# In-projection of the last 1408 tokens in seven half-size products, weight sums kept in DRAM, modulation rows later, one stream of split weights

## The chip, the cores and the metric

The kernel runs on one core of one Trainium2 chip. The metric is the device time of one execution in microseconds (us). The core has TensorE (PE, matrix products into the on-chip accumulator memory PSUM), VectorE (DVE), ScalarE (ACT), GpSimd (POOL) and SyncE (SP), which here issues every DMA. Each engine works through its own queue in order. Data lie in DRAM and in SBUF, the on-chip memory of 128 partitions; PSUM has eight banks of 512 fp32 values in each partition.

## The reference

One layer with a short gated convolution and a bidirectional mLSTM side by side, then a convolutional FFN. 128 context tokens and 2048 latent tokens pass through the same weights, with shift, scale and gate (the modulation) from two conditioning vectors.

```python
def trunk_layer(x, mod, row_len, ffn_axis, C0, n0, m0, norm1, w_in, ...):
    shift1, scale1, gate1, shift2, scale2, gate2 = jnp.split(mod, 6, axis=-1)
    h = rmsnorm(x, norm1) * (1 + scale1) + shift1
    z = h @ w_in
    sc_b, sc_c, sc_x, q, k, v, o, g = jnp.split(z, idx, axis=-1)
    u = (sc_c * sc_x).reshape(B, rows, row_len, D_CONV)
    y_sc = sc_b * conv3(u, conv_sc_w, conv_sc_b, axis=2).reshape(B, T, D_CONV)
    h_m, C, n, m = mlstm_bidir(heads(q), heads(k), heads(v), gates, C0, n0, m0)
    h_m = ... * jax.nn.sigmoid(o)
    x = x + gate1 * (jnp.concatenate([y_sc, h_m], axis=-1) @ w_out)
    h2 = rmsnorm(x, norm2) * (1 + scale2) + shift2
    up = conv3((h2 @ w_up)..., conv_ffn_w, conv_ffn_b, axis=ffn_axis)
    x = x + gate2 * ((jax.nn.silu(gg) * a) @ w_down)
```

The width is 1024, so an in-projection is a product of 1024 by 3600 (seven parts of 512 columns and 16 gate columns). `mod` is a product of 1024 by 6144 for each conditioning vector. All of it is fp32 in and out.

## The kernel before

**Tokens.** The 2176 tokens stand in one row of columns, context first, in six blocks `BL` of 384 (the last has 256). `BA` are the blocks 0 to 2 (tokens 0 to 1151) and `BB` 3 to 5 (1152 to 2175).

**Products.** An fp32 operand is split into a high part that TensorE takes exactly and a low part, the rest. A product of 128 output rows is `gemm`: for each of eight slices of 128 of the inner dimension three matmuls, high by high, high by low and low by high, 24 in all, into one PSUM bank.

```python
            PE.matmul(acc[:, :n], w_h, hH[:, k, :n], start=(k == 0), stop=False)
            PE.matmul(acc[:, :n], w_h, hL[:, k, :n], start=False, stop=False)
            PE.matmul(acc[:, :n], w_l, hH[:, k, :n], start=False, stop=(k == KT - 1))
```

`load_w` reads a weight tile of 128 by 1024 (512 KB), ScalarE copies out its high part (L105) and VectorE subtracts for the low part (L108). Three banks take turns in `accumulator`. For the gates and v (`vg`, L338 to L340) the tokens are the stationary operand and 264 weight columns stream.

**Order of the work.** (1) The start: `mod_pe` computes modulation rows 0 to 15 (shift1 and scale1) with TensorE from 16 tiles of 512 KB (L467), block 3 is read and normalised. (2) `BB`: v and gates, k and q for four heads each, the short convolution (three products per group of 128 channels), at last o. Beside them run `first_stats` (the sums of squares of `BA`) and `mod_dve`: the modulation rows 16 to 47, each from 512 KB read and two products with a sum on VectorE over 1024 elements (L510). (3) `BA`: `make_h` normalises each block beside the o products of `BB`, then `vg` and k. The scans of the gates (`gate_phase`) run beside k. (4) `weave` walks over 34 units `Sums` (state sums, backwards over the 17 chunks of 128 tokens, for two pairs of heads) and then 34 units `Mix` (the mixing itself: line L793 is part of it). Between the steps of a unit it takes products from `fill`: q, o, the short convolution of `BA` and the out-projection of blocks 0 to 3, (1, 0, 1) products per `Sums` unit and (2, 1, 2) per `Mix` unit. What is computed (k, q, o, v, sums, y) goes through DRAM (`kD`, `qD`, `oD`, `vD`, `sD`, `yD`). (5) The last out-projections, with the token sums of the FFN beside them. (6) The FFN's up-projection and (7) its down-projection.

**Seven products.** The FFN's up-projection already uses a Strassen-Winograd scheme: two output tiles by two halves of the inner dimension form a 2 by 2 weight matrix (`a11` to `a22`), two token halves by the same two halves of the inner dimension a 2 by 2 token matrix, and seven half-size products replace eight. `weights` makes the seven weight operands with four sums on VectorE (L273) and splits each (`part`, L279 and L280). Token sums are made once (`sums`) and read back (`split`). Products 0 to 2 are copied out of their bank (L957); products 2, 3, 4 and 6 accumulate onto the bank that an earlier one left; the other results are added to the copies (L964). There each product runs over two token parts of 272 columns.

**Who sets the order.** The tile framework places semaphores and puts each engine's instructions into an order of its own, by its estimates of when they are ready; the order in the text is a priority. A buffer is waited for until its last user is through.

## Time and profile before

| | |
|---|---|
| median of 3 runs | 2571.7 us (2571.41 to 2576.62) |
| the profiled execution | 2576.51 us |
| its span, first to last instruction | 2574.4 us |
| granted TensorE clock, mean | 0.992 |
| up-projection, 1086 to 2016 us | PE busy 927.1 us |
| down-projection, 2016 to 2575 us | PE busy 542.2 us |
| HBM read, written | 305.1 MB, 95.0 MB |

The page gives busy times of each engine; matmuls overlap, so their busy durations are longer than the distance from one to the next. A line such as `L200 PE MATMUL acc<-hH,wh 128*128 128x384 f32 x1280 | 440.9, 344 | 0.0` is a group: line, engine, operation, output and inputs, shape, count, then busy us and mean ns of one, and the idle time of the engine just before them with what ended it. A window's line gives the stretch, its length, busy us and count of PE, weight loads, DVE, ACT and POOL, the granted clock, the share of the DMA engines and GB/s. A DMA's line gives the tile and its source, the count, the size of one and the median us from issue to landing.

### The profile page before, as it was taken

The numbers are of one execution on the slowest core, as the hardware profiler recorded it, in microseconds if no ns is written. First come the engines' busy times: TensorE is split into PE (matmuls) and PEld (weight loads), VectorE is DVE, ScalarE is ACT, GpSimd is POOL, SyncE is SP. The second block draws the span as 40 slices with busy tenths as digits, with TensorE's granted clock in tenths as the row PEclk, the third lists the DMA queues.
The fourth block names the chain that finished last, engine by engine and source line by source line (L and its number), as shares of the span: only waits on it lengthen the run. The fifth ranks groups of instructions, "written<-read, shape, count | busy, mean of one in ns | idle before, by whom it ended". The sixth has DMA issues, their size and how long they took to land.

```text
span 2574.4 us, 46544 instructions
## 1 busy us (share of the span) xinstructions
PE 2525.0 (98%) x18511; PEld 2506.9 (97%) x18511; DVE 1621.1 (63%) x3130; ACT 1054.1 (41%) x1994; POOL 64.3 (2%) x134
## 2 busy tenths in 40 slices
PE   8999999999999999999999999999999999999998
PEld 8999999999999999999999999999999999999998
DVE  4993252332677776797887789777777635353533
ACT  4521152332444444554554455455545523231411
POOL 0000000000011110000000000000000000000000
PEclk9999999999999999999999999999999999999999
DMA  8882142565567887853252224222221826354442
GB/s 281 280 253 76 58 147 87 162 205 181 170 205 235 278 247 235 292 175 106 89 185 84 86 103 149 87 84 84 84 84 67 285 84 216 126 179 156 149 143 69
DMA packets 223579, 403.22 MB, mean 157 GB/s; under 512 B 20722, under 2 KB 144770, under 8 KB 221698
## 3 DMA queue, kind: packets, MB, share of 16 engines
q1 hardware_dynamic: 223362, 400.25, 47.4%
q8 instruction: 145, 2.38, 0.4%
q14 instruction: 72, 0.59, 0.1%
HBM read 305.13 MB, written 95.04 MB: 155 GB/s over the span
## 4 chain that ended last, share of the span: by engine, by line
PE 87%; DMA 6%; DVE 4%; issue 1%; ACT 1%; POOL 0%; SPq 0%; DVEq 0%; ACTq 0%; POOLq 0%
PE acc L200 8%; PE acc L202 8%; PE acc L201 8%; PE d L1049 7%; PE pa L952 7%; PE d L1047 7%; PE pa L954 7%; PE d L1048 7%; PE pa L953 6%; PE pb L954 3%; PE pb L952 3%; PE pb L953 3%; PE pc L954 2%; PE pc L952 2%; PE pc L953 2%; PE y L721 1%
## 5 line engine op out<-in xcount | busy, mean ns | idle before, releaser
L200 PE MATMUL acc<-hH,wh 128*128 128x384 f32 (+1 forms) x1536 | 513.3, 334 | 0.0
L202 PE MATMUL acc<-hH,wl 128*128 128x384 f32 (+1 forms) x1536 | 504.7, 329 | 0.0
L201 PE MATMUL acc<-hL,wh 128*128 128x384 f32 (+1 forms) x1536 | 503.7, 328 | 0.0
L952 PE MATMUL pa<-tH,wh 128*128 128x272 f32 x1408 | 409.0, 291 | 3.8 <-DVE row L438 3.4
L954 PE MATMUL pa<-tH,wl 128*128 128x272 f32 x1408 | 407.8, 290 | 0.1
L1047 PE MATMUL d<-uh,wh 128*128 128x272 f32 x1408 | 404.3, 288 | 2.9 <-ACT uh L996 2.2
L953 PE MATMUL pa<-tL,wh 128*128 128x272 f32 x1408 | 405.7, 288 | 0.0
L1049 PE MATMUL d<-uh,wl 128*128 128x272 f32 x1408 | 405.4, 288 | 0.0
L1048 PE MATMUL d<-ul,wh 128*128 128x272 f32 x1408 | 403.6, 287 | 0.1
L200 PEld LDWEIGHTS acc<-hH,wh 128*128 128x128 f32 x1536 | 290.1, 189 | 1.4 <-issue 0.4
L201 PEld LDWEIGHTS acc<-hL,wh 128*128 128x128 f32 x1536 | 290.1, 189 | 0.7
L202 PEld LDWEIGHTS acc<-hH,wl 128*128 128x128 f32 x1536 | 289.7, 189 | 0.3 <-issue 0.2
L952 PEld LDWEIGHTS pa<-tH,wh 128*128 128x128 f32 x1408 | 265.6, 189 | 4.5 <-DVE row L438 3.6
L1047 PEld LDWEIGHTS d<-uh,wh 128*128 128x128 f32 x1408 | 265.5, 189 | 3.7 <-ACT uh L996 2.6
L953 PEld LDWEIGHTS pa<-tL,wh 128*128 128x128 f32 x1408 | 266.1, 189 | 0.0
L954 PEld LDWEIGHTS pa<-tH,wl 128*128 128x128 f32 x1408 | 265.3, 189 | 0.3 <-DVE wl L280 0.3
L1049 PEld LDWEIGHTS d<-uh,wl 128*128 128x128 f32 x1408 | 265.0, 188 | 0.1
L1048 PEld LDWEIGHTS d<-ul,wh 128*128 128x128 f32 x1408 | 263.9, 187 | 0.5 <-DVE ul L997 0.3
L900 DVE SCALAR_TENSOR_TENSOR tt<-raw,fw,tt 128x127 f32<-128x127 f32 (+4 forms) x264 | 242.4, 946 | 4.7 <-ACT tt L906 3.6
L1008 ACT ACTIVATE wh<-st 128x1408 fp32r<-128x1408 f32 x64 | 88.3, 1380 | 356.2 <-PE d L1048 196.2
L954 PE MATMUL pb<-tH,wl 128*128 128x272 f32 x704 | 203.8, 290 | 0.8 <-DVE wl L280 0.8
L1010 DVE TENSOR_TENSOR wl<-st,wh 128x704 fp32r<-128x704 f32 x128 | 108.3, 887 | 152.5 <-ACT wh L1008 152.4
(214 smaller groups left out, 4681.8 us busy)
## 6 DMA issues: line engine op xcount, KB each, us to landing
st<-in_w_up SPq DMA_DIRECT2D x88, 512.0 KB, 4.5
st<-in_w_down SPq DMA_DIRECT2D x64, 704.0 KB, 4.1
wst<-in_w_in SPq DMA_DIRECT2D x48, 512.0 KB, 4.2
us<-uD SPq DMA_DIRECT2D x88, 272.0 KB, 4.9
R<-nD SPq DMA_DIRECT2D x34, 512.0 KB, 5.2
wm<-in_w_modr SPq DMA_DIRECT2D x32, 512.0 KB, 5.1
F<-tD SPq DMA_DIRECT2D x12, 1088.0 KB, 6.2
uD<-tt SPq DMA_DIRECT2D x22, 576.0 KB, 2.8
```

The source lines that it names most:

```text
L200: PE.matmul(acc[:, :n], w_h, hH[:, k, :n], start=(k == 0), stop=False)
L201: PE.matmul(acc[:, :n], w_h, hL[:, k, :n], start=False, stop=False)
L202: PE.matmul(acc[:, :n], w_l, hH[:, k, :n], start=False, stop=(k == KT - 1))
L900: V.scalar_tensor_tensor(o, i, w, o, op0=ALU.mult, op1=ALU.add)
L952: PE.matmul(acc, wh[:, w], rh, start=(kk == 0 and i in (0, 1, 5)), stop=False, skip_group_check=True)
L953: PE.matmul(acc, wh[:, w], rl, start=False, stop=False, skip_group_check=True)
L954: mm = PE.matmul(acc, wl[:, w], rh, start=False, stop=(kk == 3), skip_group_check=True)
L1008: S.activation(wh, st, AF.Copy)
L1010: V.tensor_sub(wl[:, a:b], st[:, a:b], wh[:, a:b].bitcast(F32))
L1047: PE.matmul(acc[b][:, :NB], wh[:, c], uh[:, q], start=(j == 0), stop=False)
L1048: PE.matmul(acc[b][:, :NB], wh[:, c], ul[:, q], start=False, stop=False)
L1049: PE.matmul(acc[b][:, :NB], wl[:, c], uh[:, q], start=False, stop=(j == FT - 1))
```

## The change

The tokens are cut anew: `BA` is blocks 0 and 1 (tokens 0 to 767), and `GR` has two groups of two equal halves: group 0 is tokens 1408 to 2175 (halves of 384), group 1 tokens 768 to 1407 (halves of 320). In both groups the in-projection goes by the seven products of the up-projection; k of group 0 alone is computed directly, as its tokens come in one half after the other. `BA` stays direct. All products now take half the inner dimension at a time.

```diff
+GR = ((1408, 384), (768, 320))
-BA = (0, 1, 2)
-BB = (3, 4, 5)
+BA = (0, 1)
+    mD = dr.tile([7, P, 4, 384], F32, name="mD")
+    wD = dr.tile([12, 4, P, WP], F32, name="wD")
...
+    def half(acc, w, s, n, first, last):
+        (wh, wl), (sh, sl) = w, s
+        for kk in range(4):
+            c = slice(kk * P, (kk + 1) * P)
+            PE.matmul(acc, wh[:, c], sh[:, kk, :n], start=first and kk == 0, stop=False, skip_group_check=True)
+            PE.matmul(acc, wh[:, c], sl[:, kk, :n], start=False, stop=False, skip_group_check=True)
+            PE.matmul(acc, wl[:, c], sh[:, kk, :n], start=False, stop=last and kk == 3, skip_group_check=True)
```

The weight operands come from one generator, in the order in which the whole kernel uses them, up-projection included. It reads up to two units ahead, and `take` keeps three split operands ahead. In group 0 the four sums of a unit are written to DRAM (`wD`); in group 1 they are read from there.

```diff
+    def seven(a11, a12, a21, a22, save=None, load=None):
+        def add(op, i, a, b, t):
+            op(t, a, b)
+            if save is not None:
+                Q.dma_start(wD[save, i][:, :n], t)
+            return t
+        if load is not None:
+            s1, s2, s4, s3 = (tmp() for _ in range(4))
+            for i, t in enumerate((s1, s2, s4, s3)):
+                Q.dma_start(t, wD[load, i][:, :n])
+            for a in (a11, s1, s2, s4, s3, a12, a22):
+                yield part(a)
+            return
+        yield part(a11)
+        s1 = add(V.tensor_add, 0, a21, a22, tmp())
+        yield part(s1)
...
+    def take():
+        while len(feed) < 3:
+            w = next(weights, None)
+            if w is None:
+                break
+            feed.append(w)
+        return feed.pop(0)
```

`pair` computes two output tiles of a group: one bank per product chain, one half-product after the other.

```diff
+        def pair(g, emit, scale=1.0, after=None):
+            t0, n = GR[g]
+            bank, cp = {}, {}
+            for i in range(7):
+                kind = KIND[i]
+                if i in (0, 1, 5):
+                    bank[kind] = pab[kind != "a"].tile([P, 512], F32, name="a" if kind == "a" else "b")
+                acc = bank[kind][:, :n]
+                half(acc, take(), gs[ORDER[i]], n, i in (0, 1, 5), True)
+                if i < 3:
+                    cp[i] = row()[:, :n]
+                    S.activation(cp[i], acc, AF.Copy, scale=scale)
+                else:
+                    m, blk, other = PLACE[i]
+                    emit(m, blk, acc, cp.get(other))
+                if after:
+                    after(i)
+                yield
```

Token sums of group 0 are made in SBUF during the start, those of group 1 by `gsums` beside group 0 (VectorE, four steps) and written to `mD`; `refill` reads them back into the seven token slots during the last pair of group 0. `fill_h` does the like with the normalised `BA` blocks during the last pair of group 1. `mod_dve` (two buffers instead of five) leaves the start's memory and is asked for beside group 1, `values` (v of `BA`), k and `fill`. The start takes the first two weight units and normalises group 0 half by half:

```diff
+            x0 = load_half(0)
+            h0 = norm_half(0, x0)
+            next(h0)
             mods(2, 4)
...
+            next(h0)
+            next(h0)
+            k3 = first_heads()
+            run(islice(k3, 1))
             mods(4, 8)
...
+            next(h0)
+            run(islice(k3, 3))
+            x1 = load_half(1)
+            h1 = norm_half(1, x1)
+            next(h1)
+            run(islice(k3, 4))
...
+        side = chain(first_stats(((768, 384), (1152, 256))), gsums(1))
+        run(beside(chain(vg(0), heads(0, qD, None, QS), heads(0, oD, AF.Sigmoid)), side, 4, 1000))
+        conv = shortconv(0, refill(1))
+        run(beside(islice(conv, 35), side, 4, 1000))
+        run(side)
+        run(conv)
...
+        run(beside(chain(vg(1), heads(1, kD), heads(1, qD, None, QS), heads(1, oD, AF.Sigmoid)), side, 6, 20))
+        run(side)
+        scale_rows()
+        run(beside(shortconv(1, fill_h), side, 6, 20))
+        run(beside(values(), side, 6, 3))
```

The mixing takes half-products instead of products:

```diff
-        weave([Sums(c, hp) for c in range(NL - 1, -2, -1) for hp in range(2)], fill, (1, 0, 1))
-        weave([Mix(c, hp) for c in range(-1, NL) for hp in range(2)], fill, (2, 1, 2))
+            weave([Sums(c, hp) for c in range(NL - 1, -2, -1) for hp in range(2)], fill, (1, 1, 1, 1, 1, 1, 1, 1, 1, 2))
...
+        weave([Mix(c, hp) for c in range(-1, NL) for hp in range(2)], fill, (2, 3, 2, 3, 2))
```

Six PSUM banks serve the groups (three and three, taken in turn), three the direct products during the mixing, as before.

More of the change, by code (lines that the diff above doesn't have):

```diff
@@ L1 @@
 from contextlib import ExitStack
-from itertools import chain, count, islice
+from itertools import chain, count, cycle, islice
 import numpy as np
@@ new lines, in values, with two @@
+                        Q.dma_start(vD[t][:, 2 * j:2 * j + 2], r)
+                        V.tensor_add(gates[:, t, j * 8:(j + 1) * 8], acc[:, 256:264], bgate[:, j * 8:(j + 1) * 8])
+                    yield
+        def two(emit):
+            for m in range(2):
+                accs = [accumulator() for b in BA]
+                for kh in range(2):
+                    w = take()
+                    for b, acc in zip(BA, accs):
+                        half(acc[:, :384], w, hs[b, kh], 384, kh == 0, kh == 1)
+                        if kh:
+                            emit(m, b, acc[:, :384])
+                        yield
+                        while due:
+                            due.pop(0)()
@@ new lines, in first_stats, with beside @@
+        def first_stats(blocks):
+            for b0, w in blocks:
+                ss = ssp.tile([P, 384], F32, name="ss")
+                for k in range(KT):
+                    x = row()[:, :w]
+                    Q.dma_start(x, I["x"][k][:, b0:b0 + w])
+                    square(ss, x, w, k == 0)
+                    if k % 4 == 3:
+                        yield
+                inv_rms(ss, w, rcol(b0, w))
+                yield
+        md = mod_dve()
+        tick = count()
+        def beside(products, side, every, mods):
+            for _ in products:
+                i = next(tick)
+                if i % every == 0:
+                    next(side, None)
+                if i % mods == mods - 1:
+                    next(md, None)
+                yield
@@ L927, in hymba_kernel @@
         cv = iter(())
-        while ahead:
-            nxt = next(prods, None)
-            if nxt:
-                ahead.append(nxt)
-            hf, j, i, (wh, wl) = ahead.pop(0)
+        for hf, j, i in ((hf, j, i) for hf in range(2) for j in range(FT) for i in range(7)):
+            wh, wl = take()
             if i == 0:
```

785 lines of the change are left out of this document (494 added, 291 removed).

## The prediction

> **What bounds the kernel now.** I read the page first: busy times, the 40 slices, the chain of work that ended last.
>
> ```profile
> span 2574.4 us, 46544 instructions
> PE 2525.0 (98%) x18511; PEld 2506.9 (97%) x18511; DVE 1621.1 (63%) x3130; ACT 1054.1 (41%) x1994; POOL 64.3 (2%) x134
> ...
> PE 87%; DMA 6%; DVE 4%; issue 1%; ACT 1%; POOL 0%; SPq 0%; DVEq 0%; ACTq 0%; POOLq 0%
> ```
>
> TensorE is on 87% of the chain that ended last, DMA on 6%, VectorE on 4%. So a matmul taken out shortens the kernel unless something else is then late. Next the windows view by stage (columns: length, then busy us of PE, PEld, DVE, ACT, POOL, granted clock, DMA share, GB/s), cut where the lines of the timeline change.
>
> ```profile
> 0.00:43.00 43.00, 33.92 (x270) 33.71 (x271) 19.53 (x53) 14.09 (x23) 1.64 (x9) 0.96 0.83 299
> 43.00:100.00 57.00, 54.96 (x423) 53.56 (x422) 42.76 (x104) 37.63 (x79) 3.28 (x17) 0.97 0.79 255
> 100.00:194.00 94.00, 94.00 (x607) 94.00 (x606) 91.33 (x172) 23.73 (x42) 4.06 (x4) 1.00 0.82 266
> 346.00:421.00 75.00, 71.30 (x548) 71.12 (x548) 31.59 (x79) 31.45 (x69) 1.43 (x14) 0.98 0.36 114
> 825.00:980.00 155.00, 144.88 (x903) 143.79 (x902) 112.70 (x340) 70.69 (x203) 17.84 (x32) 0.94 0.83 255
> 980.00:1086.00 106.00, 100.73 (x666) 100.09 (x665) 78.30 (x172) 50.38 (x102) 4.37 (x6) 0.98 0.84 274
> 1086.00:2016.00 930.00, 927.08 (x7344) 925.58 (x7343) 752.76 (x1123) 489.84 (x833) 0.44 (x1) 1.00 0.32 110
> ```
>
> TensorE idles 9.1 us in the start (43.0 − 33.9, DMA at 299 GB/s), 2.0 while it runs in, 3.7 where the last 1024 tokens hand over to the first 1152, 10.1 where the mixing units and the out-projection run together (DMA share 0.83, clock 0.94), 5.3 at the hand-over to the FFN, and 2.9 in the FFN's 930 us, which is already done in seven half-size products. In 100 to 194 VectorE is busy 91.3 us of 94 (it does the modulation rows there) and TensorE still never stops.
>
> A busy duration doesn't give the price of a matmul, since they overlap. The price is the distance between starts. One line's own view gives count, first and last start; three matmuls pass per record of a line.
>
> ```profile
> L201 PE MATMUL acc<-hL,wh x29: 334/334/343, 342.2 to 356.9; 128*128 128x384 f32 x29
> ```
> ```profile
> L201 PE MATMUL acc<-hL,wh x31: 274/283/285, 359.1 to 369.8; 128*128 128x256 f32 x31
> ```
> ```profile
> L338 PE MATMUL acc<-wh,hH x56: 281/282/290, 391.0 to 410.9; 128*128 128x264 f32 x56
> ```
>
> 14.7 us / (28 × 3) = 175.0 ns for 384 columns, 10.7 / (30 × 3) = 118.9 for 256, 19.9 / (55 × 3) = 120.6 for 264. Between the first two that is 0.438 ns a column, so 320 columns should cost 118.9 + 64 × 0.438 = 147.0 ns. Columns are what is paid for, and the weight load hides.
>
> **The change part by part.** The matmul counts of before:
>
> ```profile
> L200 PE MATMUL acc<-hH,wh 128*128 128x384 f32 x1280 | 440.9, 344 | 0.0
> ...
> L338 PE MATMUL acc<-wh,hH 128*128 128x264 f32 x272 | 79.0, 291 | 3.7 <-DVE gates L345 3.7
> ...
> L200 PE MATMUL acc<-hH,wh 128*128 128x256 f32 x256 | 72.4, 283 | 0.0
> ```
>
> *Matmuls.* A quarter of L200 is the out-projection (8 of 32 output tiles). That leaves 960 × 3 = 2880 of 384 columns and 192 × 3 = 576 of 256 for the in-projection: 2880 × 0.1750 + 576 × 0.1189 = 572.5 us. After: the first 768 tokens directly, 24 tiles × 24 × 2 blocks = 1152; k of the last 768 tokens directly, 4 × 24 × 2 = 192; the other ten pairs of tiles there, 10 × 7 products × 12 = 840; and twelve pairs for tokens 768 to 1407, 12 × 7 × 12 = 1008, of 320 columns. 2184 × 0.1750 + 1008 × 0.1470 = 530.4. v and the gates fall from 272 × 3 = 816 to 288 + 252 + 252 = 792 matmuls of 264 columns, 24 × 0.1206 = 2.9 us. **Together −45.0 us**, with every matmul on a path that TensorE sets.
>
> *Work of VectorE and ScalarE.*
>
> ```profile
> L280 DVE TENSOR_TENSOR wl<-s,wh 128x512 fp32r<-128x512 f32 x176 | 120.6, 686 | 6.1 <-ACT wh L279 2.6
> ```
> ```profile
> L510 DVE SCALAR_TENSOR_TENSOR jk<-wm,cB x64: 1222/1228/1235, 73.8 to 192.9; 128x1024 f32<-128x1024 f32 x64
> ```
> ```profile
> L380 DVE TENSOR_TENSOR cr<-acc,cr 128x384 f32<-128x384 f32 x20 | 11.1, 556 | 66.4 <-PE acc L202 66.4
> ```
> ```profile
> L279 ACT ACTIVATE wh<-s 128x512 fp32r<-128x512 f32 x176 | 111.0, 631 | 170.5 <-PE pc L953 95.0 <-PE pa L953 52.2 <-PE pb L953 18.8
> ```
> ```profile
> L377 ACT ACTIVATE cr<-acc 128x384 f32<-128x384 f32 x20 | 9.7, 483 | 52.7 <-PE acc L202 52.7
> ```
>
> A pair of 384 columns gives TensorE 7 × 12 × 0.175 = 14.7 us. VectorE does 7 splits and 4 weight sums of 512 in it (11 × 0.686) and 3 additions out of PSUM (3 × 0.556): 9.2 us, 63%; ScalarE 7 × 0.631 + 4 × 0.483 = 6.3. With the sums read back from DRAM (the 640-token group) VectorE saves 4 × 0.686 = 2.7 per pair. The short convolution adds six passes to a gated pair (3.3) and four to an output pair (2.2); statistics and token sums of the next group are 46 passes once, about 23. All this lies beside matmuls: cost 0 as long as VectorE isn't full. If that cover is gone, it is a rival below. The modulation rows, 64 × 1.228 = 79 us, leave the start's memory and queue. Line L510 began at 73.8 us, though the text issues these steps beside the q products far later: the framework starts what has its buffers. So I expect them to fill VectorE's gaps in both groups again. Their 32 reads of 512 KB move behind the first group's weights in SyncE's queue and stand there among a pair's 1 MB of weights, four saved sums of 256 KB and four stores of 192 KB: 2.9 MB in 14.7 us, 196 GB/s, below the 307 worked out further down. Weights are read up to two pairs ahead, so a late read is covered by 29 us. GpSimd only gets the same small memsets as before. Cost 0.
>
> *A new wait.* In a pair, product 2 accumulates onto the bank that product 0 left, 3 onto 1's, 4 onto 2's, 6 onto 4's. The copy or addition out of the bank has one product's time: 2.1 us (12 × 0.175), or 1.76 at 320 columns. It needs 0.483 (ScalarE) and may find a 0.631 split ahead of it: 1.1 us, in time. Or it needs 0.556 (VectorE, product 4's) and may find a 1.228 row product ahead: 1.8 us, which misses 1.76 by little. Before, three banks rotated over whole products of 4.2 us. Behind the waiting matmul stands all of TensorE's queue. Bounds over 22 pairs × 7 = 154 products: 0 (the FFN's pairs wait likewise, with three half-products between, and idle 2.9 us in 930) and 154 × 0.37 = 57 (a row product and a weight split ahead every time, 1.228 + 0.686 + 0.556 = 2.47 against 2.1). I take **+5**, near the FFN.
>
> *Start.* Two pairs of weights and one v tile (2.1 MB more than the v tile of before) now go ahead of the last eight modulation tiles: 2.1 MB / 299 GB/s = 7.0 us later. The hole can hold four of the new half-products of 2.1 us, but the second 384 tokens then wait for a normalisation of their own. Bounds: −2 (the 9.1 us of idle filled, 7.0 paid) to +12 (7.0 and half of that idle again). I take **+4**, the middle.
>
> *Hand-overs.* Slots of the next group are refilled during the last pair of the one before (`refill`, `fill_h`): seven tiles of 0.66 MB and four of 0.79 through two buffers, and for the latter 32 passes of 384, 18 us of VectorE beside the 12 us of that pair and the 35 us of v products. The like hand-over of before idles 3.7 us (346 to 421). There are two now: −3.7 to +15, I take **+1**. Entering the FFN, the stream of split weights runs on, so part of 5.3 us goes: −5 to 0, **−2**; the wait below stays, as its bank is released as before.
>
> ```profile
> PE pa L952 <- DVE row L438: 3.4, 1, 3.4
> ```
>
> *Mixing with less beside it.* The direct blocks shrink from three to two, so a mixing unit has 2.4 half-products beside it (5.0 us) instead of 5/3 products of 4.2 (7.0 us).
>
> ```profile
> L793 PE MATMUL y<-v,R x272: 273/275/422, 648.1 to 977.9; 128*128 128x129 f32 x136
> ```
>
> 33 steps in 329.8 us are 10.0 us a unit, so 3.0 of its own with the stops, some 2.7 without: 7.7 us after. Its transfers are these (DMA view of 880 to 980):
>
> ```profile
> wst<-in_w_out SPq DMA_DIRECT2D x10, 512.0 KB, 5.0
> R<-nD SPq DMA_DIRECT2D x7, 512.0 KB, 5.1
> xD<-row SPq DMA_DIRECT2D x16, 192.0 KB, 4.4
> row<-in_x SPq DMA_DIRECT2D x16, 192.0 KB, 4.6
> xt<-yD SPq DMA_DIRECT2D x3, 768.0 KB, 7.0
> sb<-sD SPq DMA_DIRECT2D x6, 258.0 KB, 3.8
> yD<-o SPq DMA_DIRECT2D x9, 128.0 KB, 3.8
> o<-oD SPq DMA_DIRECT2D x9, 128.0 KB, 3.2
> v<-vD SPq DMA_DIRECT2D x6, 129.0 KB, 4.8
> k<-kD SPq DMA_DIRECT2D x6, 128.0 KB, 4.1
> q<-qD SPq DMA_DIRECT2D x6, 128.0 KB, 2.5
> ```
>
> R, sb, v and four of 128 make 1411 KB a unit, and a half-product of the out-projection 416 KB (a quarter of weights and of four rows, 1/32 of four y tiles): 1411 + 2.4 × 416 = 2409 KB = 2.47 MB in 7.7 us, 320 GB/s.
>
> ```profile
> GB/s 281 280 253 76 58 147 87 162 205 181 170 205 235 278 247 235 292 175 106 89 185 84 86 103 149 87 84 84 84 84 67 285 84 216 126 179 156 149 143 69
> ```
>
> The stage of before moved 255 GB/s at a share of 0.83, so about 307 at 1.00. Some 22 units run so: at 307 each takes 8.0 us (+7 in all), at 285, which the page's slices hardly pass, 8.7 (+21). Of this the 10.1 us idle of before is already paid. Bounds −3 to +25 (if the units also starve each other); I take **+6**.
> The Trainium skill (Perfetto Trace Analysis, Roofline) gives a single core about 435 GB/s over its 16 DMA engines. By that, 320 GB/s would not bind and this term would be 0 or below. The trace's share of 0.83 at 255 GB/s speaks against it for transfers of these sizes, so the row decides.
>
> **Sum.** −45.0 + 5 + 4 + 1 − 2 + 6 = −31 us. The profiled execution took 2576.5 us (2.1 outside its span) and would come to 2545.5. The median of the three runs is 2571.7, 4.8 below it, so **2541 us** for the median.
>
> **The rivals.**
> 1. *All covered:* the new waits and the mixing stage cost nothing beyond before, start and FFN entry gain a little: −48, **2524 us**. For it: TensorE stands still nowhere in 100 to 194 with VectorE at 97%. Against: 320 GB/s wanted.
> 2. *Mixing bound by memory:* the 2541 with +25 in place of +6, **2560 us**. For it: clock 0.94 and 10.1 us idle there already.
> 3. *VectorE full in the 768-token group, no change:* it has 22 (v: 22 splits and sums, some 7 of additions) + 37 (q, o) + 73 (convolution) + 23 (sums) = 155 us of work in 177 us of products; 79 us of modulation rows on top make 234. If its queue puts these rows ahead of the products' additions, up to 57 us spill; with 31 more of them waited for, **2572 us**. Against: with 97% in 100 to 194 nothing waited.
> 4. *Slower, waiting for the bank:* the copy or addition out of PSUM comes late in every product, by the 0.37 us above: −45 + 57 and the other terms' 9 are +21, **2593 us**. It decides from (45 − 9)/154 = 0.23 us a product on. For it: both queues are served in order, and VectorE's is full while the modulation rows last. Against: of the two orders computed with one instruction ahead, one fits and one misses by hardly anything. The Trainium skill (TensorE: Matmul & The Clock Gate, A second HAM failure mode: psum-queue depth-cycling) reports that cycling through PSUM banks makes TensorE pause often enough that its clock drops and rises again. By it the clock row of the groups would fall below 1.00 and this case would cost more still; the FFN's window here stands at 1.00 with the same reuse at a longer distance.
> 5. *Half-size products don't come cheaper:* 320 columns cost like 384. Then 1008 × 0.028 = 28 us are lost, **2569 us**. Against: 256 and 264 columns are cheaper here by just their columns.
>
> **How the numbers follow.** A measurement of this kernel tells about 0.2% (5 us) from no change. Chances: the forecast 0.46, rival 1 0.19, rival 2 0.13, rival 3 0.08, rival 4 0.12, rival 5 0.02. The forecast and rivals 1 and 2 are faster by more than 0.2%; rivals 3 and 5 fall within 0.2% or near it; rival 4 is slower. Faster 0.79, same 0.09, slower 0.12. The range reaches from 2518 (rival 1 with its own spread) to 2570 (up to rival 3's edge); what lies outside is rival 4, most of 3 and tails, 0.2. Among the faster cases alone it would be 2520 to 2562.
>
> **What would show it.** In the profile after: 3192 in-projection matmuls of 384 and 320 columns and 792 of 264, starts 147 ns apart at 320. Waits of TensorE for a copy or addition out of PSUM under 10 us in all (rival 4: over 40, clock below 1.00 between 90 and 440 us). First v product of the Strassen group at about 86 us. VectorE below 97% in the 640-token group. The last 22 mixing units at 8 us each with DMA share over 0.9; at 7.7, rival 1; over 8.7, rival 2. I am wrong as a whole if TensorE's idle time grows by more than 40 us.

## The result, and the profile after

| | us | ratio to before, 95% interval |
|---|---|---|
| before, median of 4 runs | 2571.55 | |
| changed kernel, median of 4 runs | 2595.97 | 1.0087 [1.0063, 1.0111] |
| predicted | 2541 (2518 to 2570) | 0.988 |
| the profiled execution after | 2597.32, span 2595.2 | |

The change makes the kernel 0.9% slower. The forecast said 1.2% faster. One execution of the run e_nosave below (4756.67 us, granted clock 0.922) belongs to a slower state and is left out of its time, and its profile, which is of that execution, isn't used. The page of the changed kernel:

```profile
span 2595.2 us, 47026 instructions
PE 2502.5 (96%) x18225; PEld 2474.6 (95%) x18225; DVE 1800.9 (69%) x3431; ACT 1178.7 (45%) x2239; POOL 71.7 (3%) x136
...
PE 84%; DMA 6%; DVE 5%; ACT 2%; issue 1%; POOL 1%; SPq 0%; DVEq 0%; ACTq 0%; POOLq 0%
```

TensorE runs 286 instructions fewer, of fewer columns, and is not busy in 92.7 us of the span (2595.2 − 2502.5) where it was in 49.4 (2574.4 − 2525.0). That is +43 us, more than the 40 at which the prediction called itself wrong as a whole. The groups of products by shape and the window of a stretch without stops show that the matmuls themselves did what was forecast:

```profile
L151 PE MATMUL a<-sH,wh 128*128 128x384 f32 x664 | 236.7, 357 | 11.7 <-ACT sH L781 5.6 <-ACT sH L686 2.3 <-DMA o<-oD 1.8
...
L151 PE MATMUL b<-sH,wh 128*128 128x384 f32 x384 | 134.5, 350 | 1.4 <-ACT sH L686 1.4
L151 PE MATMUL a<-sH,wh 128*128 128x320 f32 x192 | 61.1, 318 | 10.2 <-DVE row L569 6.3 <-ACT row L495 1.6 <-DVE row L516 0.9
...
L151 PE MATMUL b<-sH,wh 128*128 128x320 f32 x144 | 44.8, 311 | 2.7 <-ACT row L495 2.7
```
```profile
400.00:450.00 50.00, 49.97 (x343) 50.00 (x343) 49.79 (x105) 24.86 (x46) 0.00 (x0) 1.00 0.80 263
```

(664 + 384) × 3 = 3144 matmuls of 384 columns, 960 of them in the out-projection, and (192 + 144) × 3 = 1008 of 320. In the 320-token group 343 of them start in 50.0 us, one each 145.8 ns. So the 45 us were saved, and over 65 us were lost again. Where, the windows show by stage (start, group 0, group 1, v of the first 768 tokens, their k and the gates, state sums, mixing with out-projection, its rest, up, down):

```profile
0.00:90.80 90.80, 74.63 (x473) 72.78 (x474) 49.88 (x98) 43.53 (x81) 2.86 (x10) 0.89 0.56 200
90.80:282.60 191.80, 185.34 (x1131) 182.01 (x1130) 169.46 (x323) 100.90 (x187) 3.18 (x14) 1.00 0.83 274
282.60:477.40 194.80, 184.22 (x1258) 180.66 (x1257) 170.83 (x353) 102.79 (x204) 3.25 (x14) 0.98 0.79 259
477.40:523.30 45.90, 39.58 (x302) 39.37 (x300) 31.04 (x72) 18.03 (x34) 0.81 (x8) 0.93 0.46 147
523.30:569.00 45.70, 45.15 (x254) 42.14 (x254) 23.28 (x81) 18.64 (x40) 0.00 (x0) 0.96 0.31 99
569.00:694.00 125.00, 125.00 (x708) 120.01 (x708) 55.99 (x123) 52.61 (x151) 0.00 (x0) 1.00 0.78 232
694.00:991.00 297.00, 275.28 (x1776) 269.85 (x1775) 228.00 (x711) 144.98 (x434) 45.86 (x70) 0.97 0.82 259
991.00:1088.80 97.80, 92.43 (x591) 91.11 (x589) 75.20 (x156) 48.83 (x95) 1.86 (x2) 0.98 0.86 287
1088.80:2034.50 945.70, 935.55 (x7427) 935.29 (x7427) 757.11 (x1125) 493.73 (x839) 2.31 (x2) 1.00 0.31 109
2034.50:2595.00 560.50, 545.27 (x4320) 541.36 (x4320) 240.13 (x396) 154.62 (x182) 11.60 (x16) 0.98 0.44 150
```
And those of before over its start, the rest of its in-projection, and all that follows up to the FFN:
```profile
0.00:97.00 97.00, 85.89 (x672) 84.27 (x673) 60.27 (x151) 49.97 (x99) 4.81 (x25) 0.96 0.80 273
97.00:428.00 331.00, 327.30 (x2193) 327.12 (x2192) 174.03 (x357) 90.22 (x165) 5.59 (x19) 0.99 0.45 142
428.00:1074.00 646.00, 630.61 (x3905) 619.83 (x3903) 389.39 (x1104) 265.10 (x711) 40.33 (x72) 0.99 0.70 216
```

Length minus PE: the start 16.2 us (before 11.1), the groups and the v products 6.5 + 10.6 + 6.3 = 23.4 (before's in-projection 3.7), from there to the FFN 27.6 (15.4), the up stage 10.2 (3.2). A stop shorter than the overlap of two matmuls (357 ns busy, 175 from start to start at 384 columns) doesn't show in PE's busy time. So for what follows I also use a finer measure, worked out from the starts in the trace: a stage's **lost time** is its length less, for every matmul, the usual distance to the next start at its shape (175 ns at 384 columns and so on).

| lost time, us | before | after | f_best (below) |
|---|---|---|---|
| start, in-projection of the last tokens, v | 24.9 | 60.9 | 51.1 |
| k of the first tokens, gates, state sums | 3.1 | 4.3 | 2.9 |
| mixing units | 18.6 | 34.0 | 19.9 |
| rest of the out-projection | 6.4 | 8.5 | 9.4 |
| stop between up and down | 0.9 | 10.3 | 3.9 |

Not all lost time is waiting. Behind its long stops TensorE runs at half its clock for a while in these traces. After the stop between up and down, which ends at 2034.4 us, the granted clock is 0.50 for 8.6 us, then 1.00:

```profile
2034.40:2043.00 8.60, 6.99 (x29) 6.68 (x30) 7.68 (x12) 5.49 (x10) 0.00 (x0) 0.50 0.89 310
2043.00:2051.60 8.60, 8.60 (x71) 8.60 (x70) 8.53 (x13) 7.52 (x12) 0.00 (x0) 1.00 1.03 378
```

In the first stretch the starts lie 227 ns apart where nothing is waited for, in the second 125, at the same 272 columns. The mean granted clock of the whole execution fell from 0.992 to 0.984. Summed over all matmuls that start at a clock of 0.50, the distance to the next start (counted at twice the usual at most) is some 24 us above the usual; before the change it was 12. So of the 66 us lost some 43 are idle time of TensorE and 12 are matmuls at half clock; the other 10 show in neither, as stops too short to count as idle would.

### The profile page after: what moved, and what is told of

It reads as the page before. It is cut to its first block, busy times and chain, and to the rows that moved or that the text cites. A ratio compares the mean times of both kernels' runs of the same rounds, so it can differ in the third digit from the quotient of the medians.

```text
span 2595.2 us, 47026 instructions
## 1 busy us (share of the span) xinstructions
PE 2502.5 (96%) x18225; PEld 2474.6 (95%) x18225; DVE 1800.9 (69%) x3431; ACT 1178.7 (45%) x2239; POOL 71.7 (3%) x136
## 4 chain that ended last, share of the span: by engine, by line
PE 84%; DMA 6%; DVE 5%; ACT 2%; issue 1%; POOL 1%; SPq 0%; DVEq 0%; ACTq 0%; POOLq 0%
PE pa L1308 7%; PE pa L1309 7%; PE pa L1310 7%; PE d L1405 7%; PE d L1403 7%; PE d L1404 7%; PE a L151 4%; PE a L152 4%; PE a L153 4%; PE pb L1309 3%; PE pb L1310 3%; PE pb L1308 3%; PE b L151 3%; PE b L152 2%; PE b L153 2%; PE pc L1309 2%
## 5 line engine op out<-in xcount | busy, mean ns | idle before, releaser
L168 ACT ACTIVATE wh<-st 128x512 fp32r<-128x512 f32 (+1 forms) x396 | 249.3, 630 | 405.1 <-PE pa L1309 119.6
L1403 PE MATMUL d<-uh,wh 128*128 128x272 f32 x1408 | 403.6, 289 | 10.1 <-ACT uh L1352 10.1
L169 DVE TENSOR_TENSOR wl<-st,wh 128x512 fp32r<-128x512 f32 (+1 forms) x396 | 272.2, 689 | 97.6 <-ACT wh L168 87.8
L151 PE MATMUL a<-sH,wh 128*128 128x384 f32 (+2 forms) x896 | 309.2, 345 | 23.1 <-DVE row L569 6.3
L152 PE MATMUL a<-sL,wh 128*128 128x384 f32 (+2 forms) x896 | 298.5, 334 | 1.2 <-DVE sL L687 0.9
L153 PE MATMUL a<-sH,wl 128*128 128x384 f32 (+2 forms) x896 | 298.6, 333 | 0.3 <-DVE wl L169 0.2
L1403 PEld LDWEIGHTS d<-uh,wh 128*128 128x128 f32 x1408 | 266.0, 190 | 10.5 <-ACT uh L1352 10.3
L1364 ACT ACTIVATE wh<-st 128x1408 fp32r<-128x1408 f32 x64 | 88.2, 1379 | 362.5 <-PE d L1404 197.8
L168 ACT ACTIVATE wh<-s 128x512 fp32r<-128x512 f32 (+1 forms) x222 | 139.8, 632 | 213.7 <-PE pc L1309 96.1
```

The lines of the kernel that those rows point to most:

```text
L151: PE.matmul(acc, wh[:, c], sh[:, kk, :n], start=first and kk == 0, stop=False, skip_group_check=True)
L152: PE.matmul(acc, wh[:, c], sl[:, kk, :n], start=False, stop=False, skip_group_check=True)
L153: PE.matmul(acc, wl[:, c], sh[:, kk, :n], start=False, stop=last and kk == 3, skip_group_check=True)
L168: S.activation(wh[:, :n], a, AF.Copy)
L169: V.tensor_sub(wl[:, :n], a, wh[:, :n].bitcast(F32))
L1403: PE.matmul(acc[b][:, :NB], wh[:, c], uh[:, q], start=(j == 0), stop=False)
```

## The experiments

The theories at the start: (A) four separate places lose the time, each a buffer or a queue that the change rearranged; (B) the transfers are full, which the change made more of (403 to 454 MB); (C) VectorE is full in the two groups. Times are medians; each ratio is to runs of the kernel before in the same series, so ratios are what compares between series.

**1. The space of the weight stream.** The waits of TensorE and SyncE's queue at the end of the up stage of the changed kernel:

```profile
PE d L1403 <- ACT uh L1352: 10.1, 1, 10.1
```
```profile
2011.76 4.14 SPq L1393 DMA_DIRECT2D ot<-xD  x7
2024.37 0.81 SPq L1361 DMA_DIRECT2D st<-in_w_down  x2
```

The last up matmul starts at 2024.1 us, and only then are the first w_down tiles asked for. Before the change that was 19 us ahead of the first down product (2016.3 us):

```profile
1997.46 0.88 SPq L1005 DMA_DIRECT2D st<-in_w_down  x2
```
The stream's pool `fp` is now the first on its side of SBUF, and the down stage's first pool lands on it.

```diff
-    fp = ph2.enter_context(tc.tile_pool(name="fp", bufs=1, side="right"))
+    fs, ft, fp = (ph2.enter_context(tc.tile_pool(name=x, bufs=1, side="right")) for x in ("fs", "ft", "fp"))
...
         dq = ph3.enter_context(tc.tile_pool(name="dq", bufs=2, side="right"))
+        dp = ph3.enter_context(tc.tile_pool(name="dp", bufs=2, side="right"))
         du = ph3.enter_context(tc.tile_pool(name="du", bufs=8, side="right"))
...
-        dp = ph3.enter_context(tc.tile_pool(name="dp", bufs=2))
```
(`st` comes from `fs`, the sums `s` from `ft`, `wh` and `wl` from `fp`; `dp` holds the prefetched outputs `ot`.)

> The changed kernel with its weight stream's tiles in three pools (sources, sums, split halves), and the down-projection's prefetch of outputs placed over the split halves, so that the first w_down loads fall on the space of sources and sums, whose last reader is a split about 9 us before the end of the up stage. Theory (space): the 10.4 us stall between the up and down stages is the wait of the first w_down load for the space of the weight stream, so the first load moves from 2024.4 us of the span to about 2015, the stall shrinks to 1 to 3 us, and the whole kernel takes 2585 to 2588 us. Rival (queue or memory): the load is late for another reason, the stall stays at 8 to 11 us, the time within 3 us of 2596.

Measured: 2584.76 us, 1.0044 [1.0028, 1.0060]. The same rows of e_down:

```profile
PE d L1403 <- ACT raw L1318: 3.2, 1, 3.2
```
```profile
2014.96 0.81 SPq L1361 DMA_DIRECT2D st<-in_w_down  x2
```

The load moved by 9.4 us, the stop fell from 10.3 to 3.3, and the down stage behind it, to its last matmul, from 553.6 to 547.0: 3 of these 6.6 us are the matmuls at half clock shown above, and 2.8 are two waits behind them (1.6 and 1.2 us). The theory holds: some 11 us of the loss (1.0087 to 1.0044) were a matter of which tiles lie on which.

**2. VectorE and the row reads.**

```diff
-        md = mod_dve()
+        md = iter(())
+        V.memset(modT[:, 16:], 0.5)
+        affine(1, 0, KT)
```

> The changed kernel without its 64 modulation row products and their 32 reads (the 32 rows behind row 15 are set to a constant). Theory (VectorE full): these 79 us of VectorE beside the two groups are why TensorE waits for weight splits, copies and the refilled slots; the idle time of the two groups falls from 26.8 us to 12 or less, that of the v products of the first 768 tokens from 9.4 to 4 or less: 2573 to 2580 us. Rival (memory): the splits are late because their sources are, the row reads are 16 MB of over 100 in that stretch, and the kernel gains 6 us or less: 2590 us or more.

Measured: 2590.37 us, 1.0055 [1.0037, 1.0074]. VectorE fell from 171 to 130 us in group 1, but the groups' lost time only from 26.7 to 21.7, and that of the v products didn't fall (9.4, now 11.1). The time is the rival's (2590 us or more); by the ratios the gain is 8 us (1.0087 to 1.0055), a little above the rival's 6, and far from what a full VectorE would give. Two runs later parted products and reads:

```diff
-                st = cj.tile([P, 1024], F32, name="wr", bufs=2)
-                Q.dma_start(st, I["w_modr"][mt - 16])
+                if mt == 16:
+                    st = cj.tile([P, 1024], F32, name="wr", bufs=2)
+                    Q.dma_start(st, I["w_modr"][0])
```

> The changed kernel with all 64 modulation row products on VectorE working on one row tile, read once (31 reads of 512 KB, 16 MB, left out; the rows behind row 16 are wrong). With products and reads left out together the two groups idled 21.7 us instead of 26.7. Theory (transfers): the reads are what cost, the groups idle 20 to 23 us here too, and the next run keeps 26 to 27. Rival (VectorE): the products cost, here the groups stay at 26 to 27 us. The whole time moves by at most 6 us from 2598.

```diff
-                t = cj.tile([P, 2], F32, name="mt", bufs=2)
-                for v in range(2):
-                    jk = cj.tile([P, 1024], F32, name="jk")
-                    V.scalar_tensor_tensor(jk, st, 1.0, cB[:, v], op0=ALU.mult, op1=ALU.mult, accum_out=t[:, v:v + 1])
-                V.tensor_scalar(modT[:, mt, :], t, bmod[:, mt:mt + 1], None, op0=ALU.add)
+                V.tensor_scalar(modT[:, mt, :], st[:, :2], bmod[:, mt:mt + 1], None, op0=ALU.add)
```

> The changed kernel with all 32 row reads, but without the 64 products of 1.22 us on VectorE (79 us; one addition of two columns stays for each row, so the rows behind row 15 are wrong). Theory (transfers): the groups' idle time stays at 25 to 28 us although VectorE falls from 170 of 192 us to about 130. Rival (VectorE): it falls to 20 to 23 us.

Measured: 2589.66 us, 1.0059 [1.0042, 1.0075], and 2589.54 us, 1.0057 [1.0042, 1.0072]; the groups lost 25.0 and 25.3 us. The three don't part: leaving out the reads, the products or both gives the same 1.0055 to 1.0059. Of the expectations only that of the transfers for e3_noop (25 to 28 us) came true; e3_nodma gave neither number. By the ratios the rows have some 8 us (1.0087 to 1.0056) of the loss, but each of the three intervals overlaps that of the changed kernel, and the groups show 1 to 5 us of it. In e3_nodma the start and the mixing stage, which the edit doesn't touch, lose some 2.5 us less each. So 8 us is an upper edge and not a measured price.

**3. The stored weight sums.**

```diff
-        units = [([pair_in(*p) for p in first], unit_heads), (vgs, unit_vg("save"))]
-        units += [([pair_in(*p)], unit_pair(save=i)) for i, p in enumerate(rest)]
+        units = [([pair_in(*p) for p in first], unit_heads), (vgs, unit_vg(None))]
+        units += [([pair_in(*p)], unit_pair()) for i, p in enumerate(rest)]
...
-        units += [([pair_in(*p)], unit_pair(load=i)) for i, p in enumerate(rest)]
+        units += [([pair_in(*p)], unit_pair()) for i, p in enumerate(rest)]
```

> The changed kernel with the weight sums recomputed in the second group, none stored or read back (26 MB of transfers less, 48 more additions of 512 or 528 on VectorE, some 33 us, in the 640-token group). Theory (VectorE full): the 640-token group holds 171 us of VectorE work in 195 us; with 33 more it is full and TensorE waits 8 to 20 us more there, 2603 to 2615 us. Rival (memory): the transfers are what the splits wait for, the first group's idle time of 10.4 us halves, the second gains as much, 2585 to 2591 us.

Measured: 2587.19 us, 1.0048 [1.0032, 1.0064]: faster than the changed kernel, as only theory B said, although VectorE has more to do. Its stages are read from the next run, which has edit 1 too.

> e_down, without storing and reading back the weight sums. The version without the other edit gained about 8 us, which only the theory of memory expected. By it the idle time of the first group (10 us) and of the second (about 20) falls to half, and the time to 2575 to 2579 us, though VectorE's busy time in the second group rises by some 30 us. Rival (the gain lay elsewhere, in the start or the FFN): the two groups together stay at 386 to 390 us.

Measured: 2576.63 us, 1.0022 [1.0010, 1.0033]. Groups 0 and 1 lose 5.7 and 15.6 us, in e_down 9.5 and 21.7.

Group 1 differs between profiles of runs that are alike up to there: from its first v product (279.7 us) on it took 197.8 us in the changed kernel, 201.0 in e_down, 204.5 in e_ahead and 204.9 in e2_wi (both below). A difference of 5 us in that stage of one profile says little; that kernels that don't store the sums lose 10 us less there (31.2 to 21.3 here) is seen again in item 7 (29.1 to 17.5).

**4. The mixing stage.** It was the term that I had priced by the transfers, so two runs tried these. First, earlier requests:

```diff
-                if i + 1 < n:
-                    units[i + 1].load()
+                for u in units[i + 1:i + 2] if not deep else units[0:2] if i < 0 else units[i + 2:i + 3]:
+                    u.load()
```

> The changed kernel with the operands of a mixing unit (k, q, v, R, state) asked for two units ahead instead of one, in the same buffers. Theory (latency): TensorE waits in the mixing stage because R and q land one unit after they are asked for, and a unit has become shorter; asked for earlier they are in time, the idle time of the stage falls from 34 us to about 20: 2580 to 2586 us. Rival (bandwidth): the 16 DMA engines are what is full there; the same bytes arrive no sooner, the stage stays at 295 to 299 us and the kernel within 3 us of 2596.

Measured: 2603.66 us, 1.0113 [1.0088, 1.0138]. The stage took 286.0 us against 288.3, lost 31.7 against 34.0; the rest of the slower time lies in group 1, which the edit doesn't touch. So late operands of the units aren't what makes the stage long. Second, fewer bytes:

```diff
-                self.R = mb.tile([P, 2, 2, 2, P], F32, name="R", bufs=3)
+                self.R = mb.tile([P, 2, 2, P], F32, name="R", bufs=3)
...
+                    for h in range(2):
+                        for d in range(2):
+                            r = 64 * d + c * 4 + 2 * hp + h
+                            S.activation(self.qs[:, h, d], R[:, h, d], AF.Exp, bias=minB[:, r:r + 1])
```

> e_down, and the mixing units read only half of R (the decay rows, 256 KB instead of 512); the other half, the weights of the carried state, are made on ScalarE by four exponentials of 128x128 a unit (34 x 256 KB = 8.9 MB fewer bytes, 42 us more ScalarE work of 297). Theory (the stage is as long as its bytes take at about 260 GB/s): 8.9 MB are 34 us; the stage from the first state product to the FFN, 391 us in e_down with 352 us of matmuls, falls by 20 to 34 us, its rate stays near 260 GB/s: 2553 to 2566 us. Rival (the chain of a unit over four engines is what is too long, whatever its bytes): four more steps on ScalarE lengthen it, the stage stays or grows: 2583 to 2600 us.

Measured: 2590.31 us, 1.0064 [1.0041, 1.0086]. The windows of the mixing units, e_down and then e2_wi:

```profile
695.70:980.20 284.50, 266.04 (x1725) 261.29 (x1725) 221.92 (x693) 141.52 (x425) 45.80 (x68) 0.97 0.84 263
```
```profile
697.90:984.70 286.80, 266.29 (x1727) 262.45 (x1725) 219.73 (x689) 176.43 (x549) 50.40 (x66) 0.96 0.78 236
```

The rate fell from 263 to 236 GB/s and the length stayed. Were the rate the limit, it would have stayed and the length fallen by 34 us. (ScalarE has 35 us more to do here, so a small gain could be hidden behind it; with the same edit the stage of e2_all, item 6, is 7 us shorter.) The waits of TensorE in e2_wi name something else:

```profile
PE a L151 <- ACT sH L686: 9.7, 2, 8.7
```

L686 splits a tile of y for the out-projection. SyncE's queue in the changed kernel shows what it follows on:

```profile
814.84 0.32 SPq L668 DMA_DIRECT2D yD<-yr  x1
...
816.80 0.41 SPq L684 DMA_DIRECT2D yt<-yD  x1
```

The convolution's last output is stored, and 2 us later the load of the same data for the out-projection's first products is issued, with its landing (4.5 us) and the split still to come. With three direct blocks the last stored one wasn't the first needed: before the change the third block's output was stored at 819.8 us, 14 us after loads for the out-projection had been issued (805.6). With two blocks the last stored ones are needed first. The test takes the store and the load out:

```diff
                     V.tensor_tensor(y, acc, y, op=ALU.mult)
-                    Q.dma_start(yD[m0 + m][:, b * 384:(b + 1) * 384], y)
+                    if (b, 0) not in yslots:
+                        yslots[b, 0] = new_slot(YS[b][0])
+                    s, k = yslots[b, 0], m0 + m
+                    S.activation(s[0][:, k], y, AF.Copy)
+                    V.tensor_sub(s[1][:, k], y, s[0][:, k].bitcast(F32))
```

> e_down without stored sums (2576.6 us), and the convolution's outputs of the first 768 tokens are split from their row tiles straight into the slots of the out-projection, instead of a store to DRAM, a load back and then the split. Theory (chain of a hand-over): the stops between 30 and 60 per cent of the mixing stage, 10 us in all beginning at 805 us in the changed kernel, are the out-projection's first products waiting for that chain of store, load and split; they fall to 4 us or less, the mixing stage's idle time from 31 to 23 to 26 us, 2569 to 2573 us. Rival (the stage is held by the transfers or the mixing chain as a whole): the stops come elsewhere, idle stays 29 to 33 us.

Measured: 2566.09 us, 0.9968 [0.9955, 0.9981], faster than the kernel before. The mixing units of e3_direct:

```profile
684.20:959.90 275.70, 264.30 (x1725) 259.45 (x1725) 220.30 (x693) 138.45 (x426) 47.73 (x68) 0.98 0.85 264
```

TensorE idles 11.4 us there (275.7 − 264.3) against 20.1 in e2_nosave, which differs by this edit alone, 21.7 in the changed kernel (288.3 − 266.6) and 10.1 before the change. In all seven profiles with this edit it idles 10.9 to 12.3 us in this stage, in the eleven of the changed kernel and its variants without it 17.0 to 22.6. So the chain of store, load and split held the stage. Only 4.6 us of the changed kernel's waits there are put down to the split itself (lines 686 and 687); that the wait for q (3.3 us in e2_nosave) went with it, and those for the decay products (line 1134) fell from 6.0 to 3.8, was seen, not explained.

**5. The hand-over to the first 768 tokens.** VectorE's queue in the changed kernel, around the 6.3 us wait of TensorE that ends at 484.3 us:

```profile
474.17 2.21 DVE L593 SCALAR_TENSOR_TENSOR F<-F,ab,rb 128x384 f32<-128x384 f32 x4 [0.31 <-DMA F<-in_x]
476.90 2.21 DVE L596 SCALAR_TENSOR_TENSOR sL<-F,modT,sH 128x384 fp32r<-128x384 f32 x4 [0.53 <-ACT sH L595]
...
479.43 1.67 DVE L593 SCALAR_TENSOR_TENSOR F<-F,ab,rb 128x384 f32<-128x384 f32 x3
481.02 1.67 DVE L596 SCALAR_TENSOR_TENSOR sL<-F,modT,sH 128x384 fp32r<-128x384 f32 x3
...
483.74 0.48 DVE L569 TENSOR_TENSOR row<-a,row 128x320 f32<-128x320 f32 x1
```

The 0.48 us addition that frees the bank stands behind the passes of `fill_h`. Two ways out of it:

```diff
+        def prep():
...
+                Q.dma_start(hD[i], x)
...
-            Q.dma_start(x, I["x"][4 * kh:4 * kh + 4, :, t0:t0 + n].rearrange("k p t -> p k t"))
+            Q.dma_start(x, hD[i])
+            put(s, x, n)
```

> e_down, and the inputs of the first 768 tokens are normalised, scaled and shifted beside the second group's products and kept in DRAM; the slots are then refilled by one copy and one subtraction of 1536 each instead of 8 passes of 384 (some 8 us of VectorE in the last pair instead of 18). Theory (VectorE's queue: the additions that free the PSUM banks stand behind the refill's passes): the 6.3 us wait for the addition of line 569 goes, 2577 to 2580 us. Rival (the refill waits for its loads or for the slots): the wait moves to the first v products, the time stays within 3 us of 2585.

Measured: 2590.05 us, 1.0066 [1.0049, 1.0084]. The v products lose 3.3 us instead of 9.4, and the groups before them 37.6 instead of 31.2, since the work and 6 MB of stores and reads went there. A wait moved, nothing gained.

```diff
+        def fill_h(i):
+            if i in (2, 3):
+                fill_b(i - 2)
+                fill_a(i)
+            elif i > 4:
+                fill_b(i - 3)
...
+        fill_a(0)
+        fill_a(1)
+        run(beside(conv, side, 6, 20))
```
(`fill_a` loads and scales, `fill_b` shifts and splits into the slots.)

> e_down without stored sums (2576.6 us), and of the four refills of the slots with the first 768 tokens the scaling of the first two is put ahead of the last pair, and the rest of each three products later, behind the additions that free the banks. Theory (order in VectorE's queue): the 6 us wait for the addition of line 569 shrinks to 1 to 3 us, the values stage idles 4 to 6 us instead of 10, 2570 to 2574 us. Rival (the work, not its place, is too much there): TensorE waits for the slots instead, idle 9 to 12 us as before.

Measured: 2573.29 us, 0.9994 [0.9981, 1.0007]. The wait for line 569 halves to 3.1 us, the stage loses 8.1 us instead of 10.1: the order was half of that wait, less than expected. The whole kernel gained 7 us on e2_nosave (1.0022 to 0.9994), of which this stage shows 2; the same edit on e3_direct gave 2 (0.9968 to 0.9960, f_best below).

**6. Four edits at once** (1, fewer bytes of R, `prep`, no stored sums):

> The four edits together (space of the stream, half of R, prepared inputs, no stored sums). If they act in different stages their gains add: 2585 - 25 - 6 - 8 = about 2546 us, below the kernel before the change. If one limit stands behind two of them (the transfer rate), less: 2555 to 2565 us.

Measured: 2576.79 us, 1.0016 [1.0005, 1.0028], the time of e2_nosave; neither expected number. The two edits that had given nothing alone gave nothing together. By stages they moved time: the mixing units are 7 us shorter than in e2_nosave (278.3 for 285.7), group 1 is 9 us longer (204.2 for 194.9).

**7. What is left with the causes taken away.** f_best has edit 1, no stored sums, the direct y and the new order of the refills.

> e3_direct with the refill order of e3_fill: space of the stream, no stored sums, convolution outputs straight into the slots, refills behind the additions. If the causes lie in different stages their gains add: 2566 - 3 = 2563 us, 0.996 of before. The forecast of 2541 is then still missed by 22 us, and these must be in the start, the groups and the mixing stage.

f_start has the second half's loads earlier:

```diff
             run(islice(k3, 1))
+            x1 = load_half(1)
             mods(4, 8)
...
-            x1 = load_half(1)
             h1 = norm_half(1, x1)
```

> f_best, and the two loads of the second 384 tokens issued before the last eight modulation tiles instead of behind them. Theory (queue): the first v product comes 4 to 8 us earlier than 90 us and the waits for the second half's statistics (1.8 and 3.2 us at 65 to 71 us) shrink; 2556 to 2560 us. Rival (work): the loads only delay the modulation tiles, which the first half needs; the first v product stays at 89 to 91 us or comes later.

> f_best with the weight sums stored and read back as in the changed kernel. Theory (stored sums cost some 12 us in the two groups): 2573 to 2577 us, groups idle 27 to 33 us against 16 to 20 of f_best. Rival (most of that gain came from spread between runs): within 4 us of f_best.

> f_best with the sums stored in the first group but computed anew in the second (the stored ones are read by nobody). If the stores cost, the first group idles 8 to 10 us as in the changed kernel, the second 10 to 14 as in f_best; if the reads cost, the first is as in f_best, 4 to 6 us, and the time is that of f_best within 3 us.

| | us | ratio, interval | groups 0 and 1, length |
|---|---|---|---|
| f_best | 2560.85 | 0.9960 [0.9944, 0.9977] | 185.7 + 190.7 |
| f_start | 2560.54 | 0.9950 [0.9937, 0.9963] | 184.2 + 191.3 |
| f_keep | 2568.25 | 0.9987 [0.9977, 0.9997] | 188.1 + 199.8 |
| f_stores | 2571.54 | 0.9995 [0.9984, 1.0006] | 187.4 + 195.4 |

f_best is 11 us below the kernel before. Stored sums cost 7.4 us (2568.25 − 2560.85), less than the 12 expected. Storing alone is no cheaper than storing and reading (so it isn't the reads), but group 1 of f_stores, which neither stores nor reads any, is 4.7 us longer than in f_best: how the cost arises isn't settled. The first v product starts at 88.6 us in f_start and at 90.9 in f_best; it was between 88.1 and 91.1 in all runs, so the queue of the loads isn't shown to matter.

Last, VectorE once more. The two groups of f_best:

```profile
90.90:276.60 185.70, 181.63 (x1116) 180.33 (x1115) 179.23 (x347) 99.64 (x185) 3.46 (x14) 1.00 0.68 221
276.60:467.20 190.60, 183.61 (x1273) 180.97 (x1271) 181.55 (x369) 103.45 (x205) 4.40 (x14) 0.99 0.58 187
```

VectorE is busy 97 and 95% of the time. So f_start without the rows, and f_start with the rows written behind the k products and the state sums (only the numbers of `beside` change).

> f_start without the 64 modulation row products and their reads (the 32 rows behind row 15 are a constant). Theory (with no sums stored VectorE is what is full in the groups: 178 of 184 us): their idle time falls from 17 to 8 us or less, 2547 to 2553 us. Rival (the stops belong to the beginning of a group, to splits, copies and hand-overs, whatever VectorE has besides): idle 13 to 17 us, 2556 to 2560 us.

> f_start with all modulation rows written behind the products of the k heads and of the sums stage, where VectorE is busy 56 us of 125. If the framework leaves them there and VectorE being full costs, the groups idle 8 us or less and the sums stage stays without idle time: 2548 to 2554 us. If the framework draws them forward into the groups again, within 3 us of 2560. If they are too much for the sums stage (56 + 60 of 125 us), that stage idles 5 us or more and the gain is lost.

Measured: 2556.53 us, 0.9929 [0.9914, 0.9943], and 2558.59 us, 0.9938 [0.9924, 0.9951]. Without the rows the groups lose 3.6 + 12.1 us, with them (f_start) 4.6 + 12.2. That is the rival's number: a VectorE that is 95% busy with work that nobody waits for costs 5 us by the ratios (0.9950 to 0.9929, intervals that overlap), 1 of them in the groups. In g_late the row products began at 107.6 us all the same, 400 us ahead of the products that they were written behind: the framework draws them into the groups again. g_late is the fastest complete version, 0.6% below the kernel before, though not clearly apart from f_start.

## Why the prediction was wrong, step by step

- **Matmuls, −45: right.** Counts as forecast, 146 ns a start at 320 columns against 147. Rival 5 is out.
- **A new wait in pairs, +5: right in kind, too low.** The waits of TensorE in the two groups, up to 480 us:

```profile
PE b L446 <- ACT wh L168: 3.6, 4, 1.6
PE b L151 <- ACT row L495: 2.7, 2, 1.7
PE a L448 <- DVE wl L169: 2.7, 2, 1.5
PE a L446 <- ACT wh L168: 2.4, 3, 1.6
PE a L151 <- ACT row L495: 1.6, 1, 1.6
PE a L151 <- DVE gates L469: 1.3, 2, 0.8
PE a L151 <- DVE row L516: 1.2, 2, 0.9
PE a L151 <- DVE row L518: 0.6, 1, 0.6
PE a L151 <- ACT wh L168: 0.5, 1, 0.5
```

  Those for copies and additions out of PSUM (lines 469 to 518) are 7.4 us. With the 6.3 of line 569, which belongs to the last pair of group 1, they are 13.7: over the 10 of the forecast, not the 40 of rival 4. That the kernel came out near rival 4's time is chance; its mechanism isn't what the time went to. The clock stands at 1.00 and 0.98 in the groups (0.50 for 3.4 us twice), so the drop that the Trainium skill (TensorE: Matmul & The Clock Gate, A second HAM failure mode: psum-queue depth-cycling) ties to cycling PSUM banks isn't what cost here.
- **Work of VectorE, ScalarE and SyncE, 0: wrong.** The step counted weights, sums and stores as 196 GB/s. The windows show 274 and 259: its 2.9 MB a pair left out the row reads, the statistics' loads and the token sums of the next group, written and read back. The stored sums cost 6 to 10 us, by the three pairs of ratios with and without them (1.0087 to 1.0048, 1.0044 to 1.0022, 0.9987 to 0.9960). A read two pairs ahead was to cover the weights; yet TensorE waited 9.2 us for their splits (lines 168 and 169 above), nearly all in the first 20 us of a group, among its v products. Rival 3 fails: the rows' work on VectorE was not the main thing TensorE waited for.
- **Start, +4: about right.** 16.2 us idle for 11.1; the first v product at 90.8 us, forecast about 86. Beside the idle time the granted clock is 0.89 there, 0.96 before: matmuls at half clock took 6 us more than usual, 3 before.
- **Hand-overs, +1: too low.** The step counted VectorE's 18 us as work beside 47 us of products, and didn't ask what stands behind them in its queue: the addition that frees a bank, 6.3 us. And it counted two hand-overs; the third, from the convolution to the out-projection, was in no term.
- **Mixing, +6: wrong cause, wrong size.** It measured 34.0 − 18.6 = +15. I priced it as bytes over a rate, 307 GB/s, which I got by raising 255 at a share of 0.83 to 1.00. 8.9 MB less should have given 34 us; they gave none in e2_wi and 7 in e2_all, so rival 2 is out, and without the convolution's way through DRAM the stage loses 21.4. Units came each 283.2 / 33 = 8.6 us after, 270.6 / 33 = 8.2 in e3_direct; forecast 8.0 at a DMA share over 0.9, where 0.82 was measured. The Trainium skill's figure (Perfetto Trace Analysis, Roofline: about 435 GB/s for a core that works alone), by which the bytes wouldn't bind, was nearer the truth than my row. Slices of the start reach 415 GB/s.
- **FFN entry, −2, and nothing behind it: right at the entry, wrong behind it.** The wait for the bank shrank from 3.4 to 1.0 us:

```profile
PE pa L1308 <- DVE row L720: 1.0, 1, 1.0
```

  But the step looked only at the entry, while the same pool, moved to the front of its side, decides what the next stage lands on: 10.3 us of stop, and a down stage 6.6 us longer than in e_down. By the ratios that is 11 us. The third hand-over above weighs as much (14 us, e2_nosave's 1.0022 to e3_direct's 0.9968).

So the forecast's largest term was right, and its list of what would then be late was too short. Of the theories at the start, A names three of the four causes (the pool's space, the refill's order, the chain through DRAM), only the stored sums speak for B, and C fails. Taking away the four causes gives 2560.85 us, 35 us below the changed kernel; 20 above the forecast remain, 16 of them in the start and the groups (51.1 − 24.9 = 26 us lost there against +10 forecast). What costs those stays open: the rows have 5 us of them at most, the place of the loads isn't it, and the waits for weight splits in the groups, still 8.3 us in f_best, were taken away by no run.

## What to carry to other kernels

When a change moves a buffer pool, look at which later stage's first loads fall on its space, and who reads the old tiles last. When a stage is shortened, list each place where one product's result is the next product's input by way of DRAM: the slack there was the work that has gone. And in an engine that serves its queue in order, a refill cut into many passes delays the short instruction behind it that a bank waits for; its share of busy time says nothing about that. And price a stop of TensorE above its length: in this kernel 24 us of matmuls at half clock came on top of 93 us of idle time.

## What was not expected of the hardware

The DMA engines' share and their rate aren't proportional. In the first 60 us of the changed kernel the rate by slices of 1.5 us is

```profile
GB/s 0 57 257 390 312 384 372 393 386 412 407 415 404 412 399 393 402 396 403 412 377 63 0 0 5 104 265 268 251 333 318 350 368 259 347 115 0 0 11 5
```

with transfers of 512 to 768 KB, while the mixing stage has 259 at a share of 0.82 with 128 to 512 KB. A window of the start beside it:

```profile
18.00:27.00 9.00, 7.12 (x59) 6.74 (x57) 3.44 (x11) 1.81 (x4) 1.25 (x1) 0.93 1.03 401
```

By the share alone the mixing stage would have 401 × 0.82 / 1.03 = 319 GB/s. To raise a rate to a share of 1.00, as I did, is not a bound.
